# Modulation columns as products on TensorE, and three gate groups traced in branch C instead of branch A

## The chip, the cores and the metric

The kernel runs on one core of one Trainium2 chip. The metric is the device time of a run in microseconds (us); lower is better. TensorE is written PE (products and transposes) and PEld (its weight loads, which overlap PE), VectorE is DVE, ScalarE is ACT, GpSimd is POOL, and SP issues most of the DMAs. A change of 0.3% of the time, about 7 us, is about what a measurement of this kernel can tell from no change.

## The reference, cut to what matters

Two layers run one after the other on 1024 tokens of width 1024; the change touches the first alone.

```python
def hybrid_layer(x, c, w_ada, b_ada, norm_g, w_in, ..., w_merge, w_br, w_out):
    mod = (jax.nn.silu(c) @ w_ada + b_ada)[:, None, :]        # c: one row of 1024, w_ada: 1024 x 3072
    shift, scale, gate = jnp.split(mod, 3, axis=-1)
    h = rms_norm(x, norm_g) * (1.0 + scale) + shift
    (a_q, a_kv, a_g, a_z, b_q, ..., d_z) = jnp.split(h @ w_in, IN_OFFSETS, axis=-1)
    y_a = nsa_attention(heads(a_q), a_kv, a_g, cmp_pos, cmp_w1, cmp_w2)
    y_b = banded_attention(heads(b_q), heads(b_k), heads(b_v), SWA_WINDOW, alibi_slopes(N_HEADS), sink)
    y_c = stick_breaking_attention(heads(c_q), heads(c_k), heads(c_v))
    y_d = retention(heads(d_q), heads(d_k), heads(d_v))
    for i, (y, z) in enumerate(((y_a, a_z), (y_b, b_z), (y_c, c_z), (y_d, d_z))):
        yi = y.reshape(B, S, BRANCH_W) * jax.nn.silu(z)
        term = jax.nn.sigmoid(h @ w_merge[i]) * (yi @ w_br[i])
        merged = term if merged is None else merged + term
    return x + gate * (merged @ w_out)
```

## The kernel before, in words

Everything is float32. A product that must be exact enough is made of three products on PE (`mm3`, lines 229 to 231): each operand is split into a high and a low part (`wh` and `wl`, `A.hi` and `A.lo`), the splits being made by ACT, DVE and POOL. The trace's wide products are those: 128 weights columns by 512 moving columns.

**The start.** `h` is kept transposed (features on partitions), so `shift` and `1 + scale` are needed as columns, 16 of them, in the tile `mod`. `ada_cols(c0)` makes two of them per call, and is called eight times (kp = 0 to 3, for `shift` and for `scale`). `ada` loads two tiles `wada` of 128 x (4 x 256) each from `w_ada` and sums the eight 128 x 256 chunks, each times its element of silu(c) (the tile `sc`), over the chunks: five of the eight on DVE (lines 455 and 458, into `adau`), three on ACT (line 451) with their sums on POOL (line 453). PE then sums each of the two partial tiles over the partitions with a column of ones (line 470, into the bank `o`): four products of one moving column a call, 32 in all. DVE adds `b_ada` (line 472) and `x_mod` turns the transposed rows of `x` into `hT`. Beside that PE does the projection of the second layer's `p` (`proj`), transposes of `x` (line 276) and `first_products` (lines 506 to 508): the first four products of branch D with the four quarters kp of `hT`, each as soon as its quarter is there. In quarter 2 the products 1 to 3 are held back by hand behind the last call of `ada_cols`. All loads of this stage go through SP in the order written (`load`). The tag `wada` has eight buffers, so the ninth load waits until the first tile has been read.

**The middle.** Branches D, A, C and B follow in this order. `attend` traces the 2 x 8 tiles (p, i) of a branch's attention, and after some tiles, by the tables `FA`, `FB` and `FC`, pieces of other work: `m` a group of the merge of the branch before, `q` the second half's set-up, `z` the gate of a head pair, `g` a call of `pre`. `pre` computes the product of `h` with one group of 256 columns of one `w_merge` ahead of time: four banks of 8 x 3 wide products, 96 in all, each bank then through a tanh on ACT and stored to DRAM (line 656), to be read back when the merge comes. `pre_todo` goes through four groups each of branches 0, 2 and 1 in this order.

**Who sets the order.** The instruction order of each engine is fixed when the kernel is built, by a scheduler that goes by priorities: the attention tiles have an early one (`stream`), the other pieces that of the place at which they were traced, and fill in where a tile has to wait. On the chip each engine then takes its instructions in that order.

Of the kernel before, what the change touches and what calls it, by code (L numbers as in the profile page):

```python
# [17 lines left out]
P = 128  # L18
# [6 lines left out]
SLOPES = [2.0 ** -2, 2.0 ** -4, 2.0 ** -6, 2.0 ** -8]  # L25
QS = 0.125

_T = dict(STA='s', XN1=0, PWT=1, PO='0x1', PO2={}, PS=2, PSX=0, PSE='a', PB=99, PEA=(0, 1, 4), WB=8, XL=3, CLO='v', STE=None, STW=None, ST1='b', ST2='b', PLP='pvv', WLO2='v', QXP=1, LW='vp', LEAD=10, FD={0: 'g', 1: 'b', 6: 'g'}, FW=(0, 2), AG=0, PREO=(0, 2, 1), PMB=0, PWB=1, PM=3, SG=2, FA={(0, 2): 'g', (0, 3): 'mmm', (0, 7): 'qm', (1, 0): 'gg', (1, 6): 'gz'}, FB={(0, 3): 'm', (0, 7): 'qm', (1, 3): 'm', (1, 5): 'z', (1, 7): 'm'}, FC={(0, 3): 'mm', (0, 7): 'q', (1, 3): 'zm', (1, 6): 'm'}, NORM='v', NORM2='v', CS=4, CSB=8, MM=2, SB=2, TB=3, OB=1, WHI='aaav', WLO='pv', PTH='a', NW=9, NBLK=31, PTB=2, XN=1, AS=(2, 4, 6, 7), CPP=2, CALT=1, WORK='s0 A A A A A A A A p s1 q t c B c B c B c B c 0a 1a P w 5 4 6 7 g 2 3a e u c B e c B c e B c c e B 1b 0b 3b', KS=(2, 0, 3, 1))


_C1 = [("trel", 1024), ("wrel", 640), ("crel", 256), ("brel", 128), ("brel2", 128), ("dm", 512), ("xi", 256), ("zeta", 256)]
# [45 lines left out]
def hybrid_then_mix_kernel(ctx: ExitStack, tc, I, c1, c2, out, dbg=None, upto=99):  # L77
# [15 lines left out]
    def blk(dt=F32, shape=(P, 1024)):  # L93
        return main.tile(list(shape), dt, name=nm("blk"), tag="blk", bufs=NBLK)
# [232 lines left out]
    def load(dst, src):  # L327
        if prev[0] is None:
            d = sy.dma_start(dst, src)
        else:  # L330
            with tc.issue_after(prev[0].ins):
                d = sy.dma_start(dst, src)
        prev[0] = d
        return d
# [101 lines left out]
    aps = obk()  # L436
    mod = main.tile([P, 24], F32, name="mod", tag="mod", bufs=1)

    def ada(c0, n, new_u, new_w, dma, side=(), new_t=None):

        u, u2 = new_u(), side and new_u()
        per = 1024 // n
        fresh = True
        for k in range(KC):
            if k % per == 0:
                w = new_w()
                dma(w[:], w_ada[:, k:k + per, c0:c0 + n])
            wk = w[:, k % per, :]
            if k in side:
                t = u2 if k == min(side) else new_t()  # L450
                ac.activation(t, wk, AF.Copy, scale=sc[:, k:k + 1])
                if k > min(side):
                    po.tensor_tensor(u2, u2, t, op=ALU.add)
            elif fresh:
                ve.tensor_scalar_mul(u, wk, sc[:, k:k + 1])
                fresh = False
            else:
                ve.scalar_tensor_tensor(out=u, in0=wk, scalar=sc[:, k:k + 1], in1=u, op0=ALU.mult, op1=ALU.add)
        return [u, u2] if side else [u]

    def st_tile(tag, bufs, shape):
        return lambda: cur[0].tile([P] + shape, F32, name=nm(tag), tag=tag, bufs=bufs)[:]

    def ada_cols(c0):

        us = ada(c0, 256, st_tile("adau", 6, [256]), st_tile("wada", _T["WB"], [4, 256]), load, _T["PEA"], st_tile("adat", 2, [256]))
        c = slice(c0 // P, c0 // P + 2)
        for m in range(2):
            for j, u in enumerate(us):
                last = pe.matmul(aps[:, c.start + m:c.start + m + 1], u[:, m * P:(m + 1) * P], ones[:], start=(j == 0),  # L470
                                 stop=(j == len(us) - 1), skip_group_check=True)
        ve.tensor_add(mod[:, c], aps[:, c], V["b_ada"][:, c])
        if c0 >= 1024:
            ve.scalar_tensor_tensor(out=mod[:, c.start + 8:c.stop + 8], in0=mod[:, c], scalar=1.0,
                                    in1=V["norm_g"][:, c.start - 8:c.stop - 8], op0=ALU.add, op1=ALU.mult)
        return last
# [33 lines left out]
    for kp in range(4):  # L510
        if kp in _T["FW"]:
            first_load(_T["FW"].index(kp))
        with stream(_T["STA"], -30000000):
            ada_cols(kp * 256)
        for c in _T["PO2"].get(kp, ""):
            if c == "x":
                x_norm(0)
            elif int(c) < _T["PS"]:
                proj(int(c), True)
        with stream(_T["STA"], -30000000):  # L520
            last = ada_cols(1024 + kp * 256)
            x_mod(0, [kp])
            if kp == 3 and _T["XN1"]:
                if _T["XL"] == 3:
                    x_load(1)
                x_norm(1)
        if kp + 10 in _T["FW"]:
            first_load(_T["FW"].index(kp + 10))
        if kp == 3:
            with tc.issue_after(last.ins):  # L530
                first_products(2, (1, 2, 3))
        first_products(kp, (0,) if kp == 2 else range(4))
        if kp == _T["XL"] and (kp < 3 or not _T["XN1"]):
            x_load(1)
    for t in proj_rows:
# [9 lines left out]
    def ada_gate():  # L545
        u = blk(F32, (P, 2, 512))
        for n in range(2):
            ada(2048 + n * 512, 512, lambda: u[:, n, :], lambda: blk(F32, (P, 2, 512)), sy.dma_start)
        gate_u.append(u)

    def ada_gate_sum():
# [1561 lines left out]
```

## Time and profile before

| | |
|---|---|
| median of 3 runs | 2320.87 us (2320.02 to 2327.75) |
| the profiled execution | 2326.91 us, of which its span is 2325.2 us |
| PE busy, share of the span | 96% |
| DVE / ACT / POOL busy | 65% / 42% / 20% |
| mean granted clock of PE | 0.985 |

The profile is of one execution, 0.26% above the median and inside the range of the three. "Busy" is the time in which an engine has an instruction under way. For PE the ends are modelled and overlap, so what a stream of products really takes is read from the distance between their starts. The granted clock is 1.00 at 2.4 GHz and 0.50 at 1.2 GHz. Whatever PE does not overlap is in the time, since it is busy 96% of it; the other engines count where PE waits for them.

### The profile page before, as it was taken

How to read it: one execution, taken by the hardware profiler on the slowest of the kernel's cores; microseconds unless marked ns; L12 is line 12 of the kernel's file. 1: busy time of each engine (PE TensorE's matmuls, PEld its weight loads, DVE VectorE, ACT ScalarE, POOL GpSimd, SP SyncE). 2: the span in 40 equal slices, each digit the busy share in tenths (PEclk: the TensorE clock that was granted, in tenths of full speed). 3: DMA queues.
4: the chain of work that ended last, by engine and by line, in shares of the span. 5: the costliest groups of instructions: out<-in, count | busy, mean ns of one | idle time of the engine just before them, and what ended most of it. 6: DMA issues, size and time to landing. Idle time of an engine off the chain costs nothing.

```text
span 2325.2 us, 30286 instructions
## 1 busy us (share of the span) xinstructions
PE 2239.4 (96%) x11004; PEld 1860.3 (80%) x11004; DVE 1517.2 (65%) x2955; ACT 966.2 (42%) x1941; POOL 474.8 (20%) x404
## 2 busy tenths in 40 slices
PE   8999999999989999999998999899999999999998
PEld 6788888888877778877887787677788888888877
DVE  7634466665677965623579876866576678578684
ACT  6211344444455544422322344634545454344452
POOL 4222100010155622112330000012034340000021
PEclk8999999999999999999999999999999999999999
DMA  9421221121132333224221211156565687525313
GB/s 319 165 90 61 63 69 50 46 89 62 32 109 84 116 119 106 73 82 145 103 71 28 82 50 37 37 172 212 159 192 180 203 324 248 176 90 163 109 55 118
DMA packets 202783, 272.72 MB, mean 117 GB/s; under 512 B 17086, under 2 KB 126214, under 8 KB 202634
## 3 DMA queue, kind: packets, MB, share of 16 engines
q1 hardware_dynamic: 194240, 257.95, 34.3%
q10 hardware_dynamic: 8394, 12.84, 1.8%
q8 instruction: 87, 1.43, 0.3%
q14 instruction: 62, 0.51, 0.1%
HBM read 199.43 MB, written 71.32 MB: 116 GB/s over the span
## 4 chain that ended last, share of the span: by engine, by line
PE 82%; DVE 9%; DMA 3%; ACT 2%; POOL 2%; issue 2%; SPq 0%; POOLq 0%; DVEq 0%; ACTq 0%
PE mm L229 15%; PE mm L230 15%; PE mm L231 15%; PE t L276 4%; PE o L823 3%; DVE blk L1342 2%; PE s L1682 2%; PE s L1684 2%; PE s L1683 2%; PE t L2028 1%; PE t L2029 1%; PE t L2027 1%; PE mm L2028 1%; PE t L1682 1%; PE mm L2029 1%
## 5 line engine op out<-in xcount | busy, mean ns | idle before, releaser
L229 PE MATMUL mm<-blk,wh 128*128 128x512 f32 x1264 | 506.2, 401 | 20.8 <-DVE tz L1157 6.2
L230 PE MATMUL mm<-blk,wh 128*128 128x512 f32 x1264 | 500.6, 396 | 0.0
L231 PE MATMUL mm<-blk,wl 128*128 128x512 f32 x1264 | 499.1, 395 | 0.3 <-DVE wl L157 0.3
L229 PEld LDWEIGHTS mm<-blk,wh 128*128 128x128 f32 x1264 | 238.7, 189 | 74.3 <-DVE tz L1157 9.2
L231 PEld LDWEIGHTS mm<-blk,wl 128*128 128x128 f32 x1264 | 238.7, 189 | 50.4 <-DVE wl L157 0.8
L230 PEld LDWEIGHTS mm<-blk,wh 128*128 128x128 f32 x1264 | 239.0, 189 | 45.9
L229 PE MATMUL mm<-wh,blk 128*128 128x512 f32 (+3 forms) x544 | 199.2, 368 | 4.3 <-DVE blk L149 1.9
L155 POOL TENSOR_TENSOR wl<-wr,wh 128x1024 fp32r<-128x1024 f32 (+1 forms) x43 | 104.5, 2431 | 465.0 <-ACT wh L147 265.4
L231 PE MATMUL mm<-wh,blk 128*128 128x512 f32 (+3 forms) x544 | 195.9, 361 | 0.3 <-DVE blk L157 0.3
L157 DVE SCALAR_TENSOR_TENSOR wh<-blk,wh 128x1024 fp32r<-128x1024 f32 x116 | 138.4, 1219 | 67.7 <-issue 59.9
L147 ACT ACTIVATE wh<-blk 128x1024 fp32r<-128x1024 f32 x116 | 117.1, 1053 | 156.1 <-PE s L2028 86.1
L230 PE MATMUL mm<-wl,blk 128*128 128x512 f32 (+3 forms) x480 | 172.2, 359 | 6.6 <-DVE wl L157 6.5
L147 ACT ACTIVATE blk<-mm 64x512 fp32r<-64x512 f32 (+3 forms) x138 | 77.8, 569 | 175.6 <-PE mm L231 112.9
L147 ACT ACTIVATE PT<-t 128x512 fp32r<-128x512 f32 (+3 forms) x224 | 96.1, 459 | 116.9 <-PE o L823 70.7
L147 ACT ACTIVATE wh<-wr 128x1024 fp32r<-128x1024 f32 (+2 forms) x95 | 97.8, 1032 | 104.4 <-DMA wr<-in_w_in_dram 25.1
L157 DVE SCALAR_TENSOR_TENSOR PT<-t,PT 128x512 fp32r<-128x512 f32 (+3 forms) x224 | 110.7, 513 | 38.9 <-ACT PT L147 38.2
L309 POOL TENSOR_TENSOR sm<-sm,mhalf 128x1 f32<-128x1 f32 x64 | 38.5, 604 | 444.0 <-DVE sm L308 425.3
L157 DVE SCALAR_TENSOR_TENSOR wl<-wr,wh 128x1024 fp32r<-128x1024 f32 (+2 forms) x76 | 96.8, 1273 | 41.1 <-ACT wh L147 18.1
L229 PEld LDWEIGHTS mm<-wh,blk 128*128 128x128 f32 x544 | 105.6, 194 | 20.7 <-DVE blk L149 2.1
L231 PEld LDWEIGHTS mm<-wh,blk 128*128 128x128 f32 x544 | 104.9, 193 | 16.2 <-DVE blk L157 1.0
L230 PEld LDWEIGHTS mm<-wl,blk 128*128 128x128 f32 x480 | 93.9, 196 | 20.4 <-DVE wl L157 8.3
L1158 POOL TENSOR_TENSOR acc<-tz,acc 128x512 f32<-128x512 f32 x48 | 67.8, 1416 | 157.7 <-DVE tz L1157 119.8
(364 smaller groups left out, 4847.5 us busy)
## 6 DMA issues: line engine op xcount, KB each, us to landing
acc<-acc SPq DMA_DIRECT2D x96, 256.0 KB, 2.6
wr<-in_w_merge_dram SPq DMA_DIRECT2D x32, 512.0 KB, 3.7
wu<-in_w_up_dram SPq DMA_DIRECT2D x32, 512.0 KB, 5.1
blk<-in_w_down_dram SPq DMA_DIRECT2D x32, 512.0 KB, 7.0
blk<-ss SPq DMA_DIRECT2D x32, 512.0 KB, 4.6
wr<-in_w_in_dram SPq DMA_DIRECT2D x27, 512.0 KB, 4.5
ss<-us SPq DMA_DIRECT2D x48, 256.0 KB, 2.3
blk<-sa SPq DMA_DIRECT2D x24, 512.0 KB, 4.4
```

The lines of the kernel that those rows point to most:

```text
L147: return ac.activation(dst, src, AF.Copy, scale=1.0 if scale is None else scale)
L155: return po.tensor_tensor(lo, x, hi.bitcast(F32), op=ALU.subtract)
L157: return ve.scalar_tensor_tensor(out=lo, in0=x, scalar=scale, in1=hi.bitcast(F32), op0=ALU.mult, op1=ALU.subtract)
L229: pe.matmul(dst, sh, mh, start=(i == 0), stop=False)
L230: pe.matmul(dst, sh, ml, start=False, stop=False)
L231: last = pe.matmul(dst, sl, mh, start=False, stop=(i == n - 1))
L276: pe.transpose(dst, src, ident)
L823: behind_pe[0] = pe.matmul(dst, v(lo + c0 + j), PT[:, j].rearrange("p a q -> p (a q)"), start=start and c0 + j == 0, stop=stop and c0 + j ...
L1158: po.tensor_tensor(acc[:], t[:], acc[:], op=ALU.add)
L1342: ve.scalar_tensor_tensor(out=acc[:, c:c1], in0=u[:, c - l:c1 - l], scalar=w, in1=acc[:, c:c1], op0=ALU.mult, op1=ALU.add)
L1682: pe.matmul(dst, wh, xh, start=first and k == 0, stop=False, skip_group_check=True)
L1683: pe.matmul(dst, wh, xl, start=False, stop=False, skip_group_check=True)
```

## The change

Two edits. First, `ada_cols` no longer sums on DVE, ACT and POOL. It loads its two `wada` tiles and lets PE make each column as eight products (one for each chunk of 128 rows, accumulated in the bank `o`): the weights are a 128 x 128 block of `wada`, the moving operand one column of `sc`. That is 16 products of one moving column a call, 128 in all, in place of 32. `ada` itself stays for the gate (`ada_gate`), on DVE alone as before. With it goes the hand-written place of quarter 2's products 1 to 3: `first_products(kp, range(4))` for all four. Second, in the tables the calls `g` that were traced after tiles (1, 0) (two) and (1, 6) (one) of branch A move to the tiles (0, 1), (0, 5) and (1, 1) of branch C. Their number and content stay.

```diff
-FA={(0, 2): 'g', (0, 3): 'mmm', (0, 7): 'qm', (1, 0): 'gg', (1, 6): 'gz'}
+FA={(0, 2): 'g', (0, 3): 'mmm', (0, 7): 'qm', (1, 6): 'z'}
-FC={(0, 3): 'mm', (0, 7): 'q', (1, 3): 'zm', (1, 6): 'm'}
+FC={(0, 1): 'g', (0, 3): 'mm', (0, 5): 'g', (0, 7): 'q', (1, 1): 'g', (1, 3): 'zm', (1, 6): 'm'}
...
     def ada_cols(c0):
 
-        us = ada(c0, 256, st_tile("adau", 6, [256]), st_tile("wada", _T["WB"], [4, 256]), load, _T["PEA"], st_tile("adat", 2, [256]))
         c = slice(c0 // P, c0 // P + 2)
+        ws = [st_tile("wada", _T["WB"], [4, 256])() for _ in range(2)]
+        for b, w in enumerate(ws):
+            load(w, w_ada[:, 4 * b:4 * b + 4, c0:c0 + 256])
         for m in range(2):
-            for j, u in enumerate(us):
-                last = pe.matmul(aps[:, c.start + m:c.start + m + 1], u[:, m * P:(m + 1) * P], ones[:], start=(j == 0),
-                                 stop=(j == len(us) - 1), skip_group_check=True)
+            for k in range(KC):
+                last = pe.matmul(aps[:, c.start + m:c.start + m + 1], ws[k // 4][:, k % 4, m * P:(m + 1) * P], sc[:, k:k + 1],
+                                 start=(k == 0), stop=(k == KC - 1), skip_group_check=True)
         ve.tensor_add(mod[:, c], aps[:, c], V["b_ada"][:, c])
...
-        if kp == 3:
-            with tc.issue_after(last.ins):
-                first_products(2, (1, 2, 3))
-        first_products(kp, (0,) if kp == 2 else range(4))
+        first_products(kp, range(4))
```

How the instructions move. **PE in the start, before**, where the sums of the second call (`adau_408`, `adau_409`) and of the third (`adau_464`) stand among the last transposes and the projection (`t` are banks of transposes, `mm` banks of the projection, `adau` the partial sums):

```order
L276 MATMUL t_287<-c_63,blk_111 128x128 x4
L276 MATMUL t_294<-c_63,blk_111 128x128 x4
L470 MATMUL o_95<-ones,adau_409 128x1
L470 MATMUL o_95<-ones,adau_408 128x1
L470 MATMUL o_95<-ones,adau_409 128x1
L229 MATMUL mm_302<-wh_103,blk_285 128x512
L230 MATMUL mm_302<-wl_104,blk_285 128x512
L229 MATMUL mm_310<-wh_103,blk_285 128x512
L230 MATMUL mm_310<-wl_104,blk_285 128x512
L470 MATMUL o_95<-ones,adau_464 128x1
L231 MATMUL mm_302<-wh_103,blk_286 128x512
```
The same place **after**, with the third call's products (line 463, on the loaded tiles `wada_460` and `wada_461`; a row with x4 is four of them):

```order
L276 MATMUL t_287<-c_63,blk_111 128x128 x4
L463 MATMUL o_95<-sc,wada_460 128x1 x4
L463 MATMUL o_95<-sc,wada_461 128x1 x4
L463 MATMUL o_95<-sc,wada_460 128x1 x4
L463 MATMUL o_95<-sc,wada_461 128x1 x4
L276 MATMUL t_294<-c_63,blk_111 128x128 x4
L229 MATMUL mm_302<-wh_103,blk_285 128x512
L230 MATMUL mm_302<-wl_104,blk_285 128x512
L231 MATMUL mm_302<-wh_103,blk_286 128x512
```
Where a call's four sums stood spread among other work, 16 one-column products now stand together, ahead of the projection's products instead of between them. After the change all eight such runs stand ahead of the first row of `first_products`; before, those of the last three calls stood among its rows.

**PE in branch A's tiles (1, 5) to (1, 7), before** (1041 and 1042 are a tile's first scores, 804 and 806 its scores, `mm` the fill with `hT` as weights):

```order
L1041 MATMUL s_5451<-kch,blk_4213 128x32
L1042 MATMUL s_5451<-kcl,blk_4213 128x32
L804 MATMUL s_5474<-blk_2261,blk_4212 128x512
L806 MATMUL s_5474<-blk_2262,blk_4212 128x512
L231 MATMUL mm_5661<-blk_602,wl_5629 128x512
L229 MATMUL mm_5661<-blk_602,wh_5628 128x512
L230 MATMUL mm_5661<-blk_603,wh_5628 128x512
L231 MATMUL mm_5661<-blk_602,wl_5629 128x512
L229 MATMUL mm_5661<-blk_663,wh_5628 128x512
L230 MATMUL mm_5661<-blk_664,wh_5628 128x512
```
The same tile's beginning, (1, 6), **after** (1031 was 1041, 794 was 804, 813 was 823, the products with the transposed probabilities `PT`):

```order
L1031 MATMUL s_5179<-kch,blk_4197 128x32
L1032 MATMUL s_5179<-kcl,blk_4197 128x32
L794 MATMUL s_5202<-blk_2245,blk_4196 128x512
L796 MATMUL s_5202<-blk_2246,blk_4196 128x512
L813 MATMUL o_4850<-PT_4993,blk_2382 128x256 x4
L276 MATMUL t_5095<-c_63,Pm_5035 128x128 x4
L813 MATMUL o_4850<-PT_5002,blk_2383 128x256
L276 MATMUL t_5107<-c_63,Pm_5035 128x128 x2
L794 MATMUL s_5206<-blk_2245,blk_4196 128x384
L796 MATMUL s_5206<-blk_2246,blk_4196 128x384
L794 MATMUL s_5211<-blk_2245,blk_4197 128x512
L796 MATMUL s_5211<-blk_2246,blk_4197 128x512
```
No row of fill is left there: from the beginning of tile (1, 5) until late in tile (1, 7) PE has only the tiles' own rows. The 288 wide products of the three groups stand behind that, among branch C's tiles.

## Rows read from the trace of the kernel before

**Rows 1.** The page: PE's busy line, and the chain that ended last, by engine.
```profile
PE 2239.4 (96%) x11004; PEld 1860.3 (80%) x11004; DVE 1517.2 (65%) x2955; ACT 966.2 (42%) x1941; POOL 474.8 (20%) x404
PE 82%; DVE 9%; DMA 3%; ACT 2%; POOL 2%; issue 2%; SPq 0%; POOLq 0%; DVEq 0%; ACTq 0%
```
**Rows 2.** Busy time of each engine in 10 us stretches of the start (columns: stretch, length, busy us and instructions, clock, DMA share, GB/s).
```profile
20.00:30.00 10.00, 9.25 (x56) 7.71 (x55) 8.52 (x12) 8.45 (x17) 4.90 (x4) 1.00 1.09 349
...
70.00:80.00 10.00, 10.00 (x51) 8.16 (x50) 5.43 (x12) 6.15 (x11) 2.92 (x4) 1.00 0.00 0
```
**Rows 3.** Groups of instructions in the first 80 us: `ada_cols` by engine.
```profile
L458 DVE SCALAR_TENSOR_TENSOR adau<-wada,sc,adau 128x256 f32<-128x256 f32 x32 | 25.7, 805 | 1.4 <-DMA wada<-in_w_ada_dram 0.6
...
L453 POOL TENSOR_TENSOR adau<-adau,adat 128x256 f32<-128x256 f32 x16 | 13.8, 868 | 5.2 <-ACT adat L451 4.3 <-PE o L470 0.7
...
L470 PE MATMUL o<-ones,adau 128*128 128x1 f32 x64 | 8.9, 252 | 0.7 <-POOL adau L453 0.7
...
L451 ACT ACTIVATE adat<-wada,sc 128x256 f32<-128x256 f32 x16 | 8.3, 528 | 0.2 <-POOL adau L453 0.2
```
**Rows 4.** PE's timeline at the full level (start, us, what, count).
```profile
28.73 0.83 PE L470 MATMUL o<-ones,adau 128*128 128x1 f32 x6 [0.75 <-POOL adau L453]
29.42 1.08 PE L276 MATMUL t<-c,blk 128*128 128x128 f32 x8
...
48.30 0.94 PE L470 MATMUL o<-ones,adau 128*128 128x1 f32 x8
49.11 0.48 PE L506 MATMUL mm<-blk,wh 128*128 128x512 f32 x1
...
70.07 0.39 PE L506 MATMUL s<-blk,wh 128*128 128x512 f32 x1
70.30 0.39 PE L507 MATMUL s<-blk,wh 128*128 128x512 f32 x1
```
**Rows 5.** PE's timeline while the clock was at its lower level.
```profile
32.12 1.28 PE L470 MATMUL o<-ones,adau 128*128 128x1 f32 x6
33.26 0.77 PE L229 MATMUL mm<-wh,blk 128*128 128x512 f32 x1
```
**Rows 6.** Stretches with small products: PE busy and granted clock.
```profile
27.70:31.10 3.40, 2.65 (x24) 2.34 (x22) 2.69 (x6) 3.40 (x9) 1.99 (x3) 1.00 1.09 348
48.20:51.50 3.30, 3.11 (x22) 2.48 (x20) 2.76 (x6) 3.30 (x8) 1.60 (x3) 1.00 0.97 322
249.80:253.40 3.60, 3.60 (x64) 3.60 (x63) 0.00 (x0) 0.00 (x0) 0.00 (x0) 1.00 0.00 0
```
**Rows 7.** Stretches at the lower level in the start.
```profile
31.10:37.90 6.80, 6.80 (x25) 5.80 (x23) 6.20 (x13) 4.84 (x11) 3.76 (x5) 0.50 1.09 348
...
51.60:58.40 6.80, 5.69 (x13) 4.46 (x14) 6.80 (x12) 3.85 (x7) 5.17 (x6) 0.50 1.00 346
...
82.30:85.70 3.40, 2.97 (x11) 2.63 (x12) 2.90 (x5) 2.49 (x4) 1.38 (x1) 0.50 0.59 164
```
**Rows 8.** The loads of `wada` (shortest, median, longest issue; first and last start).
```profile
L332 SPq DMA_DIRECT2D wada<-in_w_ada_dram x16: 1257/1418/2491, 11.0 to 38.9; - x16
```
**Rows 9.** Branch A's tiles (1, 5) to (1, 7): busy time of each engine.
```profile
533.00:615.00 82.00, 82.00 (x438) 70.22 (x437) 49.49 (x157) 36.50 (x86) 13.07 (x8) 1.00 0.18 55
```
**Rows 10.** The same stretch by lines: one of three lines of wide products; DVE's weight splits.
```profile
L231 PE MATMUL mm<-blk,wl 128*128 128x512 f32 x83 | 33.0, 397 | 0.0
...
L157 DVE SCALAR_TENSOR_TENSOR wl<-wr,wh 128x1024 fp32r<-128x1024 f32 x3 | 3.7, 1226 | 2.6 <-PE mm L230 2.3
```
**Rows 11.** A later stretch, of the second layer, in which DVE sets the pace.
```profile
1440.00:1480.00 40.00, 35.84 (x166) 26.26 (x165) 38.22 (x115) 27.66 (x61) 2.61 (x4) 0.90 0.07 27
```
**Rows 12.** Branch C's tiles, and two stretches at the lower clock in it.
```profile
640.00:840.00 200.00, 183.97 (x1027) 156.68 (x1026) 152.61 (x214) 105.30 (x232) 104.04 (x103) 0.97 0.31 97
693.40:696.60 3.20, 3.20 (x11) 2.81 (x12) 3.02 (x4) 1.62 (x4) 2.00 (x2) 0.50 0.35 101
754.80:761.40 6.60, 5.91 (x19) 4.50 (x20) 6.43 (x8) 2.71 (x6) 6.18 (x6) 0.50 0.54 178
```

More of the change, by code (lines that the diff above doesn't have):

```diff
@@ L26 @@
 QS = 0.125
-_T = dict(STA='s', XN1=0, PWT=1, PO='0x1', PO2={}, PS=2, PSX=0, PSE='a', PB=99, PEA=(0, 1, 4), WB=8, XL=3, CLO='v', STE=None, STW=None, ST1='b', ST2='b', PLP='pvv', WLO2='v', QXP=1, LW='vp', LEAD=10, FD={0: 'g', 1: 'b', 6: 'g'}, FW=(0, 2), AG=0, PREO=(0, 2, 1), PMB=0, PWB=1, PM=3, SG=2, FA={(0, 2): 'g', (0, 3): 'mmm', (0, 7): 'qm', (1, 0): 'gg', (1, 6): 'gz'}, FB={(0, 3): 'm', (0, 7): 'qm', (1, 3): 'm', (1, 5): 'z', (1, 7): 'm'}, FC={(0, 3): 'mm', (0, 7): 'q', (1, 3): 'zm', (1, 6): 'm'}, NORM='v', NORM2='v', CS=4, CSB=8, MM=2, SB=2, TB=3, OB=1, WHI='aaav', WLO='pv', PTH='a', NW=9, NBLK=31, PTB=2, XN=1, AS=(2, 4, 6, 7), CPP=2, CALT=1, WORK='s0 A A A A A A A A p s1 q t c B c B c B c B c 0a 1a P w 5 4 6 7 g 2 3a e u c B e c B c e B c c e B 1b 0b 3b', KS=(2, 0, 3, 1))
+_T = dict(STA='s', XN1=0, PWT=1, PO='0x1', PO2={}, PS=2, PSX=0, PSE='a', PB=99, PEA=(0, 1, 4), WB=8, XL=3, CLO='v', STE=None, STW=None, ST1='b', ST2='b', PLP='pvv', WLO2='v', QXP=1, LW='vp', LEAD=10, FD={0: 'g', 1: 'b', 6: 'g'}, FW=(0, 2), AG=0, PREO=(0, 2, 1), PMB=0, PWB=1, PM=3, SG=2, FA={(0, 2): 'g', (0, 3): 'mmm', (0, 7): 'qm', (1, 6): 'z'}, FB={(0, 3): 'm', (0, 7): 'qm', (1, 3): 'm', (1, 5): 'z', (1, 7): 'm'}, FC={(0, 1): 'g', (0, 3): 'mm', (0, 5): 'g', (0, 7): 'q', (1, 1): 'g', (1, 3): 'zm', (1, 6): 'm'}, NORM='v', NORM2='v', CS=4, CSB=8, MM=2, SB=2, TB=3, OB=1, WHI='aaav', WLO='pv', PTH='a', NW=9, NBLK=31, PTB=2, XN=1, AS=(2, 4, 6, 7), CPP=2, CALT=1, WORK='s0 A A A A A A A A p s1 q t c B c B c B c B c 0a 1a P w 5 4 6 7 g 2 3a e u c B e c B c e B c c e B 1b 0b 3b', KS=(2, 0, 3, 1))
 _C1 = [("trel", 1024), ("wrel", 640), ("crel", 256), ("brel", 128), ("brel2", 128), ("dm", 512), ("xi", 256), ("zeta", 256)]
@@ L437, in hybrid_then_mix_kernel, with ada @@
     mod = main.tile([P, 24], F32, name="mod", tag="mod", bufs=1)
-    def ada(c0, n, new_u, new_w, dma, side=(), new_t=None):
-        u, u2 = new_u(), side and new_u()
+    def ada(c0, n, u, new_w, dma):
         per = 1024 // n
-        fresh = True
         for k in range(KC):
@@ L448, in ada @@
             wk = w[:, k % per, :]
[L449 to L454, printed above, removed]
+            if k == 0:
                 ve.tensor_scalar_mul(u, wk, sc[:, k:k + 1])
-                fresh = False
             else:
                 ve.scalar_tensor_tensor(out=u, in0=wk, scalar=sc[:, k:k + 1], in1=u, op0=ALU.mult, op1=ALU.add)
-        return [u, u2] if side else [u]
     def st_tile(tag, bufs, shape):
@@ L547, in ada_gate @@
         for n in range(2):
-            ada(2048 + n * 512, 512, lambda: u[:, n, :], lambda: blk(F32, (P, 2, 512)), sy.dma_start)
+            ada(2048 + n * 512, 512, u[:, n, :], lambda: blk(F32, (P, 2, 512)), sy.dma_start)
         gate_u.append(u)
```

## The prediction

> **What bounds the kernel now.** I read the page first: PE is busy 96% of the span, and 82% of the chain that ended last is PE's own work [rows 1]. So the question for each edit is what it adds to PE's stream, and what idle time of PE it fills or opens. Next I read the start in stretches of 10 us: after the first 20 us PE is busy 9.25 of 10 us between 20 and 30 us, and all of 70 to 80 us [rows 2]. DVE, ACT and POOL carry the modulation sums there: 25.7 us on DVE's largest line, 13.8 on POOL, 8.3 on one of ACT's two lines [rows 3]. PE waits for them little (the column idle before, and a first wait of 0.75 us in [rows 4]). The timeline then gives prices: six records of one-column products take from 28.73 to 29.42, 0.115 us each; eight from 48.30 to 49.11, 0.101 each; a wide product 0.23 [rows 4]. A product of this kind has two records: 64 for the 32 products [rows 3]. At the lower clock six take from 32.12 to 33.26, 0.19 each [rows 5].
>
> **Edit one, what it removes.** All of the sums on DVE, ACT and POOL. I cost this at nothing: PE is the engine waited for. Only where PE waited for that chain does it pay: 0.75 us before the first sums and some such waits later, about 2 us in all.
>
> **Edit one, what it adds.** 128 products in place of 32 are 192 more records on PE. At 0.101 to 0.115 us that is 19.4 to 22.1 us; I take 0.110, nearer the six in a row among small work, so **+21 us**. Nothing hides it: PE has 0.75 us of idle time in 20 to 30 us and none in 70 to 80 us [rows 2].
>
> **Edit one, the clock.** The granted clock fell at 31.1 us and at 51.6 us, to half, for 6.8 us each, and at 82.3 us for 3.4 us [rows 7]. Ahead of the first fall stood 24 records, of transposes and one-column products; ahead of the second 22, of which 16 were one-column products [rows 6]. In the second stretch PE was busy 3.11 of 3.30 us, so it fell without the engine having stood idle long. The change makes eight runs of 32 one-column records, each 32 x 0.11 = 3.5 us long, with nothing wide in them. I therefore expect the clock to fall at most of the eight. The second and third runs stand among transposes with no wide product between them: 64 one-column records (7 us) and 28 transposes (eight from 29.42 to 30.45 in the same rows: 0.13 each, 3.6 us) take 10.6 us at the full level and 0.19 / 0.11 times as much at the lower one [rows 4, 5], 7 us more. The other six are each followed by 6 to 12 wide products; a fall of the shortest length seen, 3.4 us, loses half of it, 1.7 us, one of 6.8 us loses 3.4 us; five falls at 2.6 us are 13 us. Together **+20 us**, between 0 (the clock stays up) and 31 us (the whole stretch from the first run, at about 23 us, to the last, at about 85, at the lower level, half of it lost). The two old falls at 31.1 and 51.6 us, 13.6 us long, lie inside this count, so their loss of **-7 us** goes off. Behind the start I give back **-4 us**: the 2 us of waits above, and part of the fall at 82.3 us, since the second half of `x` and the gate's sums will be further along when PE comes later. That part could be 0 to 7.
>
> The TensorE page of the Trainium skill ("TensorE: Matmul & The Clock Gate", the section "Why this matters for your kernels") lays a drop of the clock in mid-kernel to gaps in which PE is idle. By that, an engine that only loads weights and streams single columns keeps its clock, and these 20 us would be nothing. The stretch from 48.20 to 51.50, in which PE was busy almost throughout before the fall, does not agree with it [rows 6].
>
> The loads are not late. The last of the 16 began at 38.9 us [rows 8]. They now wait for PE to have read a tile eight loads before instead of for ACT, and so move back to about the fourth run, at 50 to 60 us; the eighth run stands behind all of the projection, later than 70 us. Even 10 us from issue to use leaves them hidden; without that cover the seventh or eighth run would wait some us each, which the range holds. Each run begins behind DVE's addition of the run before; DVE is freer than it was. Quarter 2's products move ahead of their place with no change of number, at no cost.
>
> So the start: 21 + 20 - 7 - 4 = **+30 us**, from +10 to +45.
>
> **Edit two.** The three groups are 288 wide products, 288 x 0.23 = 66 us of PE, and 12 tanh, 12 stores and six loads of weights, which go with them. In branch A's last three tiles, 82 us, PE is busy throughout, with 83 wide products on one of their lines [rows 9, 10] and 82 on each of the two others: 247 x 0.23 = 57 us of fill and 25 us of the tiles' own work. In the new order these tiles have no fill. They cannot run in 25 us: DVE has 49.5 us of work in the same 82 us, 3.7 of it the splitting of the fill's weights [rows 9, 10]. Where DVE sets the pace it is busy 38.2 of 40 us [rows 11]; 45.8 us at that rate are 48 us, and the last of it lies beside fill again, since that returns late in tile (1, 7): I take 45. So PE stands idle about 20 us where it was never idle, between 0 (PE's pace) and 27 (all 49.5 us count: 52 us at that rate).
>
> Against that stands branch C. Between 640 and 840 us PE is busy 184.0 of 200 us, so 16 us idle, and 10 us of low clock lose 5 [rows 12]: at most 21 us to win with 66 us of fill. But its waits are for a tile's chain of POOL, DVE and ACT, and stay where the fill stands in the wrong place; the order after has long pure stretches of fill in C and still stretches with as little of it as before. I take half, 10 us, with 0 and 21 as the bounds. **+20 - 10 = +10 us**, from -10 to +25. The stores go to the same queue, SP, in C; reading back follows merges that come later still, so none is late.
>
> **Sum.** 30 + 10 = +40 us on the profiled execution, 2326.9 us, gives 2367. The profile lies 6 us above the median of the runs shown, 2320.9, so on that the forecast is **2361 us**. Its own range: start +22 to +45 and exchange 0 to +20, 2343 to 2386.
>
> **The rivals.**
> - *The clock stays up in the one-column runs.* For it: 64 records of small products from 249.80 to 253.40 us, 3.6 us in one run, did not lower it [rows 6], but these stream 32 columns each, not one. Then the start costs 21 - 7 - 4 = +10, and with +10 from edit two the time is 2341.
> - *Branch C takes all the fill it can, and A's tiles lose half of what I think.* 21 us won in C, 10 lost in A: with the start's +30 the time is 2321 + 19 = 2340. For it: C's 21 us are there to be had [rows 12]. Against it: A's DVE needs 45 us where PE needs 25.
> - *Faster: the exchange decides.* A's last tiles run at PE's pace, none of the 57 us of fill having covered anything, and C's idle time and low clock all go: -21. It makes the kernel faster by over 7 us only where the start costs under 14 us, so only with the clock up as well: 10 - 21 = -11, 2310. Against it are DVE's 49.5 us in the tiles.
> - *No change that can be told.* 2314 to 2328 needs the clock up, so +10 in the start, and C to win about 10 us more than A loses.
>
> **How the numbers follow.** Forecast 0.70; clock up 0.16; C takes all 0.07; exactly offset 0.03; faster 0.04. The likeliest is 2361. Below its own range lie the first two rivals, at 2341 and 2340; taking most of them in, and the upper bounds (+45 and +25 together are 2391) in part, the range is **2330 to 2388**. A difference of 0.3%, 7 us, is what a measurement can tell from none: slower than 2328 are the first three cases, 0.92 with a little off their edges; within, 0.05; faster 0.03.
>
> **What would show it.** Right: in the first 100 us, 256 records of one-column products at 0.11 us or 0.19 us; a granted clock of 0.50 for 35 to 50 us in all there, against 17 us in the three stretches of [rows 7]; the last row of `first_products` some 30 us or more behind its old end at 78 us; DVE's and POOL's lines of `adau` gone with no gain; in A's tiles (1, 5) to (1, 7) PE idle with DVE near 95%; in C fewer idle us. Wrong, if the clock stays at 1.00 through the runs, if A's tail takes under 35 us, or if C's idle time does not fall at all, which would add 10 us.

## The result

The changed kernel takes 2376.03 us (median of 4 runs, 2372.52 to 2381.28) against 2321.22 us before: a ratio of 1.0232, 95% interval 1.0204 to 1.026. That is slower, as forecast, by 55 us where 40 were forecast; the time lies inside the range.

The page of the profile after, PE's busy line and the chain that ended last, beside [rows 1]:

```profile
PE 2284.9 (96%) x11196; PEld 1897.0 (80%) x11196; DVE 1479.1 (62%) x2915; ACT 956.8 (40%) x1917; POOL 452.5 (19%) x388
PE 83%; DVE 9%; DMA 4%; ACT 2%; issue 1%; POOL 1%; SPq 0%; DVEq 0%; POOLq 0%; ACTq 0%
```

PE has exactly 192 instructions more and is still busy 96% of a longer span; DVE lost 38 us of work, and the kernel is not faster for it. Where the time went is read by laying both traces side by side at the same instruction:

| instruction | before, us | after, us | shift |
|---|---|---|---|
| first tile of branch A, its first scores (PE) | 278.9 | 308.0 | +29.1 |
| tile (1, 5) of branch A | 533.7 | 559.3 | +25.6 |
| first scan of branch C (DVE) | 630.8 | 612.8 | -18.0 |
| first softmax maximum of branch B (DVE) | 839.8 | 887.7 | +47.9 |
| second layer, last `fl` copy (DVE) | 1285.2 | 1333.6 | +48.4 |
| second layer, last `wl` split (DVE) | 1629.8 | 1684.0 | +54.2 |
| end of the span | 2325.2 | 2379.5 | +54.3 |

So three places carry it: the start (+29), the exchange between branches A and C (+19), and a stretch of the second layer that neither edit touches (+6).

The start after: PE's timeline (start, us, what, count), at the full level and at the lower one, beside [rows 4, 5]:

```profile
30.25 3.63 PE L463 MATMUL o<-sc,wada 128*128 128x1 f32 x32
33.75 2.42 PE L276 MATMUL t<-c,blk 128*128 128x128 f32 x12
35.95 6.83 PE L463 MATMUL o<-sc,wada 128*128 128x1 f32 x32
42.64 1.09 PE L276 MATMUL t<-c,blk 128*128 128x128 f32 x4
43.38 0.78 PE L229 MATMUL mm<-wh,blk 128*128 128x512 f32 x1
43.96 0.63 PE L230 MATMUL mm<-wl,blk 128*128 128x512 f32 x1
44.38 0.63 PE L231 MATMUL mm<-wh,blk 128*128 128x512 f32 x1
```

From start to start 32 records take 3.50 us at the full level, 0.109 each, and 6.69 at the lower one, 0.209 each; the wide products behind them take 0.42. All 256 are one group (columns as in [rows 3]), with no idle time of PE before any of them, so no load of `wada` was late:

```profile
L463 PE MATMUL o<-sc,wada 128*128 128x1 f32 x256 | 39.8, 289 | 0.0
```

Stretches after (columns as in [rows 2]): four lines of the start, beside [rows 2, 7]; then branch A from its first half's last tile to the first scan of branch C, and branch C from there to branch B's first tile; the end of branch A, beside [rows 9, 11]; the stretch of the second layer:

```profile
20.00:30.00 10.00, 10.00 (x68) 8.99 (x67) 0.57 (x2) 5.25 (x10) 2.38 (x1) 1.00 1.09 348
50.00:60.00 10.00, 10.00 (x42) 9.42 (x43) 0.32 (x2) 1.19 (x2) 0.00 (x0) 0.50 0.71 245
34.20:68.30 34.10, 34.10 (x139) 31.78 (x138) 3.32 (x8) 6.67 (x10) 2.35 (x1) 0.50 0.73 247
20.00:140.00 120.00, 119.55 (x592) 104.61 (x591) 42.44 (x75) 35.06 (x56) 20.73 (x17) 0.80 0.54 178
476.81:612.78 135.97, 123.90 (x685) 103.46 (x683) 94.87 (x344) 67.91 (x184) 13.26 (x9) 0.97 0.12 35
612.78:887.72 274.94, 259.32 (x1378) 218.26 (x1379) 163.42 (x234) 124.74 (x264) 106.04 (x111) 0.99 0.30 95
559.00:600.00 41.00, 29.12 (x175) 22.22 (x174) 37.46 (x150) 26.53 (x71) 3.18 (x3) 0.97 0.00 1
1333.55:1683.99 350.44, 329.33 (x1576) 266.18 (x1576) 244.28 (x545) 150.19 (x327) 30.28 (x32) 0.96 0.30 97
```

The same stretches in the trace before, between the same instructions:

```profile
20.00:80.00 60.00, 57.86 (x281) 48.08 (x279) 44.65 (x77) 35.87 (x68) 26.40 (x25) 0.89 0.77 256
20.00:140.00 120.00, 114.25 (x625) 98.53 (x624) 75.97 (x145) 48.88 (x93) 40.94 (x37) 0.91 0.59 193
447.67:630.76 183.09, 183.09 (x985) 156.93 (x984) 109.80 (x355) 82.24 (x206) 20.66 (x13) 1.00 0.19 60
630.76:839.77 209.01, 192.98 (x1079) 164.59 (x1078) 158.51 (x223) 109.72 (x240) 106.08 (x108) 0.98 0.30 93
1285.18:1629.77 344.59, 324.31 (x1576) 263.00 (x1576) 248.51 (x545) 151.00 (x327) 30.72 (x32) 0.98 0.31 99
```

The reader is to see four things. Between 34.2 and 68.3 us PE was busy every moment and its clock was at half throughout. In 20 to 140 us the mean clock fell from 0.91 to 0.80: at half level for (1 - 0.80) x 2 x 120 = 48 us against 22. Branch A became 47.1 us shorter, though 66 us of fill left it, and PE now stands idle 12.1 us there. And branch C became 65.9 us longer, the whole of the fill, with PE idle 15.6 us as against 16.0: it took none of the fill into its idle time. What PE waits for at the end of branch A (559 to 600 us; line waited at, what for, us, times, longest) is DVE, in every wait that the trace names there; the two largest:

```profile
PE o L813 <- DVE PT L157: 6.5, 4, 4.4
PE s L794 <- DVE mx L835: 3.4, 4, 2.3
```

### The profile page after: what moved, and what is told of

Its sections match the earlier page's. It is cut to its first block, busy times and chain, and to the rows that moved or that the text cites. A ratio compares the mean times of both kernels' runs of the same rounds, so it can differ in the third digit from the quotient of the medians.

```text
span 2379.5 us, 30550 instructions
## 1 busy us (share of the span) xinstructions
PE 2284.9 (96%) x11196; PEld 1897.0 (80%) x11196; DVE 1479.1 (62%) x2915; ACT 956.8 (40%) x1917; POOL 452.5 (19%) x388
## 4 chain that ended last, share of the span: by engine, by line
PE 83%; DVE 9%; DMA 4%; ACT 2%; issue 1%; POOL 1%; SPq 0%; DVEq 0%; POOLq 0%; ACTq 0%
PE mm L229 16%; PE mm L230 16%; PE mm L231 15%; PE t L276 4%; DVE blk L1332 3%; PE o L813 2%; PE s L1672 2%; PE s L1674 2%; PE s L1673 2%; PE o L463 2%; PE t L2018 1%; PE t L2019 1%; PE t L2017 1%; PE mm L2018 1%; PE mm L2019 1%; PE t L1672 1%
## 5 line engine op out<-in xcount | busy, mean ns | idle before, releaser
L229 PE MATMUL mm<-wh,blk 128*128 128x512 f32 (+3 forms) x544 | 201.9, 373 | 4.0 <-DVE wh L149 1.1
L231 PE MATMUL mm<-wh,blk 128*128 128x512 f32 (+3 forms) x544 | 199.0, 367 | 0.3 <-DVE blk L157 0.3
L147 ACT ACTIVATE wh<-wr 128x1024 fp32r<-128x1024 f32 (+2 forms) x95 | 97.7, 1031 | 118.6 <-DMA wr<-in_w_in_dram 22.4
L230 PEld LDWEIGHTS mm<-wl,blk 128*128 128x128 f32 x480 | 94.6, 197 | 22.1 <-DVE wl L157 8.8
```

The costliest lines, as they stand in the source:

```text
L147: return ac.activation(dst, src, AF.Copy, scale=1.0 if scale is None else scale)
L229: pe.matmul(dst, sh, mh, start=(i == 0), stop=False)
L230: pe.matmul(dst, sh, ml, start=False, stop=False)
L231: last = pe.matmul(dst, sl, mh, start=False, stop=(i == n - 1))
```

## The experiments

The times are medians; each ratio is to the kernel before, measured beside it on the same chip, with its 95% interval.

**Either edit alone.** The tables of before with the new `ada_cols`, and the tables of after with the old one.

```diff
 # e1_cols_only: the changed kernel with
-FA={..., (1, 6): 'z'}, FC={(0, 1): 'g', (0, 3): 'mm', (0, 5): 'g', ...}
+FA={..., (1, 0): 'gg', (1, 6): 'gz'}, FC={(0, 3): 'mm', (0, 7): 'q', ...}
 # e2_gates_only: the kernel before with the opposite exchange
```

> Edit one alone: the modulation columns as one-column products, the three gate groups where they were, in branch A. Theory (the two edits cost apart and add up): the start costs what it cost in the changed kernel, a shift of about +29 us at the first tile of branch A, and no exchange follows, so 2321 + 29 = 2350 us, or 2356 if the 6.5 us lost between 1325 and 1530 us in the changed kernel hang on the start too. The granted clock is 0.50 for 40 to 50 us of the first 100. Rival (the exchange is the larger part, and the start's delay is given back where branch A's tiles have fill): under 2340 us.

> Edit two alone: the three gate groups traced in branch C, the modulation sums as before. Theory (they add up): no shift before 480 us; branch A ends some 49 us earlier and branch C some 18 us later than before, so 2321 + 18 = 2339 us, and 2345 if the 6.5 us of the second layer belong to this edit. PE is idle in branch A's last tiles with DVE busy 90 to 95%. Rival one (the forecast's take-back in branch C, which the late start spoiled): 2331. Rival two (the groups' place doesn't matter): 2321, within 7 us.

Measured: 2357.37 us, 1.0141 (1.0117 to 1.0166), for edit one; 2349.77 us, 1.0105 (1.0073 to 1.0136), for edit two. The excesses add up to 2.46%, between the changed kernel's 2.32% and the 2.56% of its second measurement (below), so the edits act apart, as far as intervals of a quarter of a per cent to either side can tell. By these ratios edit one costs 33 us, where 29 or 35 were expected, and edit two 24, where 18 or 24 were. Edit one's trace is +27.4 us at branch A's first tile and +28.5 at branch B's, and ends at +29.7. Edit two's trace: branch A 137.9 us, branch C 275.5. Both of the second edit's rivals fall: the late start didn't spoil a gain in branch C, there is none, and it matters in which branch the groups stand.

```profile
451.42:589.36 137.94, 126.52 (x685) 106.62 (x683) 95.75 (x344) 67.96 (x184) 13.26 (x9) 0.95 0.12 35
589.36:864.90 275.54, 260.11 (x1378) 219.53 (x1379) 163.69 (x234) 124.83 (x264) 107.14 (x111) 0.98 0.31 95
```

**The clock by itself.** The same 128 products, but the moving operand is the column repeated 64 times (`WC` is 64); of each 64 equal results one is read. In the changed kernel, and with edit one alone. Cut to what matters:

```diff
+    scw = cur[0].tile([P, KC, WC], F32, name="scw", tag="scw", bufs=1)
+    for k in range(KC):
+        ve.tensor_scalar_mul(scw[:, k, :], ones[:, 0:1].to_broadcast([P, WC]), sc[:, k:k + 1])
...
-                last = pe.matmul(aps[:, c.start + m:c.start + m + 1], ws[k // 4][:, k % 4, m * P:(m + 1) * P], sc[:, k:k + 1],
+                last = pe.matmul(aps[:, o + m * WC:o + (m + 1) * WC], ws[k // 4][:, k % 4, m * P:(m + 1) * P], scw[:, k, :],
...
-        ve.tensor_add(mod[:, c], aps[:, c], V["b_ada"][:, c])
+        ve.tensor_add(mod[:, c], aps[:, o:o + 2 * WC:WC], V["b_ada"][:, c])
```

> The changed kernel, with each modulation product streaming the same scalar column 64 times (64 columns in place of one) into 64 columns of the bank, of which one is read. Theory one (the clock falls because the runs stream next to nothing): the granted clock stays at 1.00 through the runs, the products' records stay near 0.11 us, since the weights' load sets them, and the start's shift is +8 to +13 us in place of +29, so 2376 - 18 = 2358 us. Theory two (loading fp32 weights in runs is what lowers the clock, whatever is streamed): the granted clock falls as before, the shift is +29 us or more, 2376 to 2385. Theory three (64 columns cost what they save): clock at 1.00, but records of 0.2 us, so +30, 2376.

> The same 64 streamed columns, with the three gate groups left in branch A: edit one alone with (by theory one) the clock kept up. Theory one: 2321 + 10 = 2331 us, the records' bare price. Theory two: as edit one alone, 2350 or more. If the start turns out cheaper than the sums that it replaced, under 2321.

Measured: 2359.44 us, 1.0156 (1.013 to 1.0182), in place of 1.0232; and 2337.41 us, 1.0059 (1.0041 to 1.0077), in place of 1.0141. The timeline and the stretch of `e3_wide64`:

```profile
31.72 3.68 PE L468 MATMUL o<-scw,wada 128*128 128x64 f32 x32
35.24 1.48 PE L276 MATMUL t<-c,blk 128*128 128x128 f32 x12
```

```profile
20.00:140.00 120.00, 118.44 (x758) 105.75 (x757) 49.82 (x99) 38.45 (x67) 23.99 (x20) 1.00 0.56 186
```

32 records take 3.52 us, 0.110 each: 63 more columns cost nothing that shows, and the clock is 1.00 from 20 to 140 us, where it was 0.80. The shift at branch A's first tile is +7.7 us in place of +29.1 (and +8.3 in place of +27.4 with edit one alone). Theory one holds; loading weights in runs doesn't lower the clock by itself. The Trainium skill ("TensorE: Matmul & The Clock Gate", the section on LDWEIGHTS) gives a load of 128 weight columns as columns / 1.2 in ns, 107 ns, whatever the rows. An estimate by that, with a new load for each record, is 0.107 us a record; the 0.109 and 0.110 us at the full level agree with it, though the records of the loads themselves last 0.19 us each and overlap. What the low clock cost is the difference, 19 to 21 us in the traces, 17.6 and 19.0 in the ratios (0.76% and 0.82%).

**The same trick in the kernel before.** Its 32 products with 64 columns of ones (cut to the product).

```diff
-                last = pe.matmul(aps[:, c.start + m:c.start + m + 1], u[:, m * P:(m + 1) * P], ones[:], start=(j == 0),
+                last = pe.matmul(aps[:, o + m * WC:o + (m + 1) * WC], u[:, m * P:(m + 1) * P], onesw[:], start=(j == 0),
```

> The kernel before, with its 32 modulation products (the sums on DVE, ACT and POOL as they were) streaming 64 columns of ones in place of one. Theory (the low clock at the start comes from the one-column products): the falls at 31.1 and 51.6 us go, 13.6 us of low clock less, so about -7 us, 2322 - 7 = 2315 us, and a granted clock of 1.00 from 20 to 80 us. Rival (those falls come from the transposes and from PE's waits between them): the falls stay, 2322 us, within 3.

Measured: 2322.34 us, ratio 1.0000 (0.9991 to 1.0009). In the trace:

```profile
20.00:80.00 60.00, 56.12 (x288) 45.67 (x287) 47.09 (x82) 36.36 (x70) 26.82 (x26) 0.97 0.79 262
20.00:140.00 120.00, 113.97 (x648) 96.60 (x648) 80.11 (x150) 50.86 (x97) 41.89 (x38) 0.99 0.61 202
```

The falls went in this trace as the theory says (0.99 for 0.91), yet the expected time didn't come. PE's waits don't account for it: from 20 to 140 us PE is idle 6.0 us in place of 5.8, and the wait for the sums themselves (on POOL's `adau`) is 0.7 us in both traces. But the falls at 31.1 and 51.6 us are no fixed property of that code. Of the seven traces with this start unaltered (before, and six with other tables: one above, five below), four have a mean clock of 0.89 from 20 to 80 us and three 0.94 to 1.00. The six reach the row of branch A at which the stretches above begin (447.67 us before) between 441.86 and 451.42 us, `e5_sums_wide64` at 443.60. The one that came first, `e12_early_moved`, had its clock up from 20 to 80 us without any change, and PE idle 4.9 us:

```profile
20.00:80.00 60.00, 55.06 (x291) 44.68 (x290) 47.15 (x84) 37.84 (x72) 27.19 (x27) 1.00 0.81 271
```

So the 4.1 us that the trace of `e5_sums_wide64` gains there are inside what the unchanged start does by itself. The granted clocks of all runs say the same: over the whole kernel the mean is 0.9896 in the eleven runs with 64 columns and 0.9891 in the fifteen of the kernel before beside them, while the two traces differ by 0.990 to 0.985.

**Half the products.** As `e3_wide64`, with every second chunk only: half of each modulation sum is left out.

```diff
-            for k in range(KC):
+            for k in range(0, KC, 2):
```

> The changed kernel with 64 streamed columns, and only four of the eight products of each modulation column (half of each sum is left out, so the outputs are not the reference's). Theory (each record costs its bare 0.115 us, and nothing hides it): 128 records fewer, -14.7 us: 2359 - 15 = 2344 us, and a start ahead of the kernel before's by 6 to 8 us. Rival (a part of the records lies in time in which PE would have waited for the normalisation of x anyway): -5 to -8 us, 2352.

Measured: 2341.96 us, 1.0092 (1.0071 to 1.0112), 0.64% or 15 us less than `e3_wide64`, by the theory; at branch A's first tile it stands 5.6 us ahead of the kernel before (6 to 8 were expected), 13.3 ahead of `e3_wide64`. 128 records less at 0.110 us are 14.1. The records cost their bare price; nothing hides them.

**The exchange, group by group.** All with the old `ada_cols`: first one of the three groups moved to branch C, the one at tile (1, 6); then two; then one again, but an early one, from tile (1, 0).

```diff
 # before: FA (1, 0): 'gg', (1, 6): 'gz'; FC no 'g'
 # e6_one_moved:    FA (1, 0): 'gg', (1, 6): 'z';  FC (0, 1): 'g'
 # e7_two_moved:    FA (1, 0): 'g',  (1, 6): 'z';  FC (0, 1): 'g', (1, 1): 'g'
 # e12_early_moved: FA (1, 0): 'g',  (1, 6): 'gz'; FC (0, 1): 'g'
```

> The kernel before with one of the three gate groups moved to branch C, tile (0, 1), and two left in branch A at tile (1, 0). Theory one (branch A's last tiles need some 20 to 25 us of fill for DVE's pace, and three groups bring 66): branch A ends 22 us earlier and stays without idle time on PE; branch C gains nothing of its idle time and ends where it did, so 2322 us, within 4. Theory two (each group costs a third of what three cost): branch A ends 15 us earlier, 2322 + 9 = 2331 us. Rival (branch C takes the first group into its idle time): 2312 to 2318.

> The kernel before with two of the three gate groups moved to branch C, tiles (0, 1) and (1, 1), and one left in branch A at tile (1, 0). Theory one: the one group left, 22 us, is about what branch A's last tiles can use, so most of the cost comes only with the third: branch A ends 40 to 44 us earlier, 2322 to 2328 us. Theory two (in proportion): 2322 + 18 = 2340 us.

> One of the three gate groups moved to branch C, tile (0, 1), as in the run with one group moved, but here it is one of the two that stood at branch A's tile (1, 0); the other stays there and the group at tile (1, 6) stays in its place. Modulation sums as before. Theory (PE takes fill as it comes, so what stands at tile (1, 0) is used up long before branch A's last tiles, and only the group at tile (1, 6) covers these): PE is busy throughout in branch A, which ends 22 us earlier instead of 15, its PE idle time is under 1 us instead of 4.5, and branch A and branch C together take 392 to 395 us against 400.6 with the late group moved and 392.1 before: 2322 to 2327 us. Rival (each group moved costs about 8 us, whichever it is): 2334 us, 400 us for the two branches.

Measured: 2333.61 us, 1.0051 (1.0038 to 1.0064); 2347.08, 1.0107 (1.0092 to 1.0122); 2334.02, 1.0047 (1.0029 to 1.0066). Branch A and branch C in the traces, one fence for each kernel in this order:

```profile
449.34:617.45 168.11, 163.64 (x887) 139.91 (x886) 104.16 (x351) 77.76 (x200) 18.20 (x12) 0.99 0.16 51
617.45:849.97 232.52, 215.48 (x1178) 181.75 (x1178) 162.19 (x226) 113.78 (x247) 104.03 (x109) 0.99 0.30 94
```

```profile
444.53:596.19 151.66, 143.52 (x783) 121.94 (x782) 104.10 (x350) 72.87 (x193) 15.81 (x11) 0.98 0.14 42
596.19:855.01 258.82, 239.49 (x1281) 203.07 (x1281) 157.34 (x228) 118.78 (x253) 100.76 (x110) 0.97 0.30 93
```

```profile
441.86:610.94 169.08, 164.60 (x887) 140.88 (x886) 103.99 (x351) 77.99 (x200) 18.22 (x12) 0.98 0.16 51
610.94:843.33 232.39, 215.46 (x1178) 181.58 (x1178) 160.43 (x226) 113.95 (x247) 105.53 (x109) 0.99 0.30 94
```

| groups moved | branch A, us | PE idle in A | branch C, us | PE idle in C | A and C |
|---|---|---|---|---|---|
| none | 183.1 | 0.0 | 209.0 | 16.0 | 392.1 |
| one, late | 168.1 | 4.5 | 232.5 | 17.0 | 400.6 |
| one, early | 169.1 | 4.5 | 232.4 | 16.9 | 401.5 |
| two | 151.7 | 8.1 | 258.8 | 19.3 | 410.5 |
| three | 137.9 | 11.4 | 275.5 | 15.4 | 413.5 |

My theory that the end of branch A needs only one group is refuted: with two groups left PE is idle 4.5 us there, with one left 8.1. The other theory, that the late group is the one that counts, was not tested, for the two tables with one group moved built the same kernel: PE's 11004 instructions stand in the same order in both traces, by line and tile name. In both the two groups that stay are worked off in the same place: their last tanh on ACT begins 97 us after the row at which these stretches begin (at 546.4 and at 538.9 us), against 128.9 (at 576.6) with all three in branch A. The two runs are one kernel measured twice, and differ by 0.4 us in the medians and 0.9 in A and C together. Fill is put in from the front, wherever a tile waits, so each group less bares another piece at the end, and there DVE sets the pace.

The groups do not cost alike. At 22.1 us of fill each, the first, second and third cost branch A 7.1, 5.6 and 8.4 us. Branch C grew by 23.5, 26.3 and 16.7 us. Together that is 8.5, 9.9 and 3.0 us, and by the medians the third cost nothing that can be told (1.0107 with two moved, 1.0105 with three). A price in proportion, theory two of both runs, fits the time with one moved (2331 us expected) and is too low with two (2340 expected). With all three moved, A and C together take 410.9 to 413.5 us in the seven traces that there are. Why the second lengthened branch C by more than its own work and the third by less is not shown.

**Branch C's idle time.** All three groups in branch C, with the projection for its second pair of heads ahead of the second group; and with the gate groups behind the merge's groups.

```diff
 # e2_gates_only: FC (0, 1): 'g', (0, 3): 'mm', (0, 5): 'g', (0, 7): 'q', (1, 1): 'g', (1, 3): 'zm', (1, 6): 'm'
 # e8_q_first:    FC (0, 1): 'g', (0, 3): 'mm', (0, 5): 'q', (0, 7): 'g', (1, 1): 'g', (1, 3): 'zm', (1, 6): 'm'
 # e9_g_for_m:    FC (0, 0): 'mm', (0, 2): 'g', (0, 4): 'g', (0, 7): 'q', (1, 0): 'zm', (1, 3): 'g', (1, 6): 'm'
```

> All three groups moved to branch C, modulation sums as before; in branch C the projection for its second pair of heads is traced at tile (0, 5) and the second gate group at (0, 7), the two places exchanged. Theory (branch C regained nothing because the second group's products stand ahead of that projection, so that 50 us of fill lie between the last tile of the first pair and the first of the second, with DVE and POOL nearly idle): that stretch shrinks by about 22 us, the products lie beside the second pair's tiles, and branch C regains 5 to 10 us: 2350 - 7 = 2343 us. Rival (PE's own work is the sum either way, and the idle time in the last tiles of each pair is DVE's and POOL's pace): 2350 us, within 4.

> All three gate groups in branch C and the modulation sums as before, as in the run with edit two alone, but in branch C the merge's groups are traced ahead of the gate groups: merge, merge at tile (0, 0), gate groups at (0, 2), (0, 4) and (1, 3), the merge's third group at (1, 0). Theory (branch C keeps its 16 us of idle time because what stands beside its last tiles is the merge, whose sums DVE and POOL must do, the two that set the pace there; a gate group needs ACT alone): with gate groups there PE's idle time in branch C falls from 15.4 us to 8 or 10, and the time from 2350 to 2342 to 2344 us. Rival (PE waits there for the tiles' own chain, and any fill leaves the same idle time): 15 us of idle time, 2350 us, within 4.

Measured: 2338.73 us, 1.0071 (1.0057 to 1.0085), and 2343.22, 1.0097 (1.0071 to 1.0124). Set beside edit two alone (2349.77 us), the one time is better than the gain expected and the other looks like it; by their traces neither is that gain. Branch C of the one and of the other:

```profile
579.88:856.57 276.69, 262.17 (x1378) 220.59 (x1379) 165.13 (x234) 124.11 (x264) 99.41 (x111) 0.98 0.30 94
```

```profile
582.01:857.28 275.27, 258.74 (x1378) 219.91 (x1379) 169.44 (x234) 123.20 (x264) 105.59 (x111) 0.98 0.30 94
```

It takes 276.7 and 275.3 us as against 275.5, and PE is idle in it 14.5 and 16.5 us as against 15.4. So neither where the projection stands nor which kind of fill stands beside the last tiles sets this idle time; both theories fall. The better time of `e8_q_first` has to come from elsewhere: in its trace the start is 4.2 us ahead of before, which the edit doesn't touch, and the second layer's stretch shorter (below), in one trace of each. What PE waits for in branch C of `e9_g_for_m` (the three largest, columns as above):

```profile
PE mm L229 <- DVE tz L1157: 7.5, 4, 4.6
PE t L276 <- DVE Pm L1115: 2.6, 1, 2.6
PE mm L229 <- DVE blk L157: 2.2, 1, 2.2
```

Here it is largely the fill itself that waits, for a bank that DVE has still to read (line 1157 is the merge's multiplication). Before and in the changed kernel it is the tiles, some 10 us, more than the fill, 5 to 6 us, in waits of 2.1 us at most, nearly all on DVE.

**The changed kernel once more.**

> The changed kernel once more, unaltered. Theory (the 6.5 us lost between 1325 and 1530 us, which neither edit touches, come from falls of the clock whose places differ from execution to execution): low clock from 1200 to 1600 us differs from the 34.1 us of the first profile by 7 us or more, and the loss with it; the start's low clock stays between 42 and 52 us. Rival (they belong to the kernel's order): 34 us of low clock there again, and the same loss of 6 to 7 us. Time 2376 us, within 4, either way.

Measured: 2380.14 us, 1.0256 (1.0232 to 1.028).

```profile
20.00:140.00 120.00, 119.55 (x613) 104.49 (x612) 44.95 (x77) 36.86 (x59) 21.86 (x19) 0.83 0.54 180
1331.78:1682.64 350.86, 329.12 (x1576) 265.14 (x1576) 244.56 (x544) 150.16 (x327) 30.87 (x32) 0.97 0.29 97
```

The start has its low clock again (0.83: 41 us at half) and the second layer's stretch its loss, 6.3 us (350.9 for 344.6), so the rival holds: the loss comes back with the kernel. In the other twelve traces this stretch takes 340.8 to 348.1 us, with edit one alone 345.1, with edit two alone 347.7. No edit touches its code, but the order built for it changed: PE has the same 1576 instructions there before and after, in another order (by line and tile name), and both executions of the changed kernel have the order of after. How much the order is worth is not known closely, since four traces with one order among them took 344.8 to 347.7 us, and four with another 342.5 to 345.9. PE is busy 5 us longer at a mean clock of 0.96 or 0.97 in place of 0.98, which is a part of it; `e8_q_first` takes 340.8 there at 0.97, so the mean clock doesn't tell all. What in the order calls these falls forth stays open.

## Why the prediction was right, and where it was not

- **The direction and the start were right, by its steps.** The forecast for the start was +30 us; the trace shows +29.1. Its terms: 192 records at 0.110 us, measured 0.109 at the full level, so 21. Low clock of 35 to 50 us in the first 100: measured 48, against 22 before from 20 to 140 us, so 24 us lost less 11, a net 13, which is the forecast's 20 - 7 with both terms some 4 us larger. Given back: PE's idle time from 20 to 140 us fell from 5.8 to 0.5 us, 5.3 where 4 was taken. 21 + 13 - 5.3 = 29. The shape was otherwise than taken: not a short fall behind most of the runs, but 34.1 us in one piece, through the wide products between the runs as well, and shorter falls behind it. A record at the lower level took 0.209 us, where 0.19 was read from six; and the sum for the second and third runs, 10.6 us at 0.19 / 0.11 times, comes to 7.7 us more, not 7.
- **The clock's rival fell, and its price was tested by itself.** With the clock kept up the start costs +7.7 to +8.3 us; that rival said +10. The Trainium skill's rule that the prediction weighed against it, a clock lost to gaps in which PE is idle ("TensorE: Matmul & The Clock Gate", "Why this matters for your kernels"), doesn't describe this case: PE was busy 10.00 us from 20 to 30 us, ahead of the fall, and 34.10 of the 34.10 us at half level.
- **The credit of -7 for the old falls was weaker than the prediction took it to be.** It came from one execution: the same start varies by 9.6 us from one execution to another (441.86 to 451.42), and with the falls gone from the trace no time was won that can be told. That the sum came out so close is luck in this: the profiled execution of before stood near the middle of these.
- **The removed sums were worth little, as "about 2 us" says.** 5.3 us of PE's idle time went with them; with the clock kept up, so that PE is not late for another reason, 4.2 (1.6 us left in `e3_wide64`). Waits named as for the sums were 0.7 us of it, and what caused the rest was not tested. Against 21 us of records it is little either way.
- **The loads stayed hidden**: no idle time before any of the 256 records.
- **Branch A's loss was right in size and cause, not in its parts.** The forecast was a loss of 20 us, all of it PE standing idle at DVE's pace. 66 us of fill left and the branch became 47.1 us shorter, a loss of 19. Of these 12.1 are idle time; the clock, 0.97 over 136 us where it was 1.00, is 4 more; 3 us are not accounted for. In 559 to 600 us DVE was busy 37.5 of 41 us, 91% where near 95% was the sign, and PE 29.1.
- **The step that failed is "I take half, 10 us" for branch C.** It regained nothing: 65.9 us longer for 66 us of fill, PE idle 15.6 us where it was 16.0, which the prediction named among its signs of being wrong, at 10 us. It had its reason in hand, that C's waits "stay where the fill stands in the wrong place", and still took half of the bound between two ends. Two other orders of the fill left it at 14.5 and 16.5 us, so the idle time isn't a lack of fill. That PE takes its instructions in the built order, so that one waiting for DVE holds up the fill behind it, would account for it; no run here took DVE's work away, so this is argued and not shown. The failed step is 10 of the 15 us by which the forecast was low.
- **Not foreseen: 6 us in the second layer**, the rest of the miss. It came again in the second trace of the changed kernel, in an order that neither edit names; how the order makes it is unexplained.

No version tried beats the kernel before; the nearest, its own products with 64 columns, equals it.

## What to carry to other kernels

Work moved from idle engines onto the engine that bounds the kernel cost its full price here, however small each piece; before moving such work, ask what that engine's clock does while it streams next to nothing, and pad the moving side if its columns are free. Fill counts only where it stands beside a wait, so price its leaving by the end of the stage, where the pace passes to another engine, and take no gain from its arrival until a trace shows idle time that fill has shortened. Idle time of the bounding engine is no reserve as such: see first whether what it waits for is work, or the engine that must empty its banks. And read the order that was built, not the table: two tables here built one and the same order, and an edit of the first layer changed the order of the second.

## What was not expected of the hardware

A product of 64 fp32 columns took the time of one with a single column (0.110 and 0.109 us a record, each with 128 x 128 weights), and runs of the first kept the clock at 1.00 where runs of the second, with PE busy without a break, held it at 0.50 for 34.1 us. And the same start, with PE's instructions in the same order, had a mean clock from 20 to 80 us of 0.89 in one profiled execution (before) and 1.00 in another (`e12_early_moved`).
